# A two-layer decoder trunk for a prompt and eight samples: streams mixed by steps of one projection, samples' work in halves

## The chip, the cores and the metric

One core of a Trainium2 chip. The metric is the device time of one launch in microseconds (us). TensorE is PE below (PEld its weight loads), VectorE DVE, ScalarE ACT, GpSimd POOL; SP issues most of the DMAs. Every engine works through its own list of instructions in order and waits for semaphores of the others.

## The reference, cut to what matters

The trunk has two layers. It runs for a prompt of 1024 tokens and for 8 sample tokens that share all weights.

```python
def mem_attend(q, mk, mv):
    s = jnp.einsum('blhd,bmhd->bhlm', q, mk) * (q.shape[-1] ** -0.5)
    return jnp.einsum('bhlm,bmhd->blhd', jax.nn.softmax(s, axis=-1), mv)

def a_mixer(hn, w_in, lb, hg_gain, mem_k, mem_v, w_o, s0):      # layer 0
    q_h, f_h, i_h, g_h, q_m = jnp.split(hn @ w_in, 5, axis=-1)
    ...
    o, S = hgrn2_scan(q, k, v, logf, s0)       # state: S = f * S + k v, output q S
    o = rmsnorm(o, hg_gain) * jax.nn.silu(g_h)
    om = mem_attend(q_m, mem_k, mem_v)
    return jnp.concatenate([o, om], axis=-1) @ w_o, S

def b_mixer(...):                                               # layer 1
    os_ = stick_breaking(q_s, k_all, v_all, bias, q_pos, k_pos)
    om = mem_attend(q_m, mem_k, mem_v)
    return jnp.concatenate([os_, om], axis=-1) @ w_o

for l in range(DEPTH):
    hn = rmsnorm(h, g[0])
    mix = ...                                   # a_mixer or b_mixer
    h = h + rmsnorm(mix, g[1])
    h = h + rmsnorm(swiglu(rmsnorm(h, g[2]), w_gu[l], w_down[l]), g[3])
```

The samples have their own caches: 256 rows of memory keys and values each, a 128x128 state for each of 4 heads, and 256 past positions of the shared keys and values. The width is 1024, the inner width of the feed-forward part (FFN) 2816.

## The kernel before, in words

The prompt is cut into two groups of 512 tokens, 0 and 1; the 8 samples ride along as extra columns of group 1 (its matmuls are 260 columns wide, two of them for one of 512). Weights, and most activations, are split into a high and a low half (`ws`, by L208 on ACT and L209 on DVE, from a tile `w` that SP loads in L203), and a product of 128x128 weights is three matmuls. `proj` (L214 to L225, matmuls in L222) is one such projection: 24 matmuls of 512 columns for 8 blocks of input. Its result stands in one of two buffers `mm`; DVE and ACT take it out (`silu` with L247, L250 and L251, the gating product L819 and L230).

The order of the work is written as generators. Each `yield` ends a step, and `weave` (L178) always takes the next step of the stream that has made the smallest share of its weight: with weights 30, 50 and 24, for example, the three streams make 30, 50 and 24 steps in the same stretch. The instructions are recorded in that order and then placed on each engine by a scheduler; `tc.issue_after(split[0].ins)` tells it to place an instruction on DVE behind the last weight split made so far (L209, or L573 for Strassen slices).

The parts that the change touches:

- `ffn` (L800) computes the FFN by plain projections; a step of `part` is a gate and an up projection. `ffn_w` (L660) computes slices by Strassen's scheme: `gate_up_w` (L528) loads blocks with L538 into raw tiles, some of which lie in the buffers `b` that the attention parts use too, adds them on DVE (L557 to L565), splits them in L571 (ACT) and L573 (DVE) and multiplies in L578; its down projection is L751.
- `sample_scores` (L1037): for each sample a key tile `c` and a broadcast query row `b<-qd` are loaded, multiplied on DVE (L1057) and summed over each head (L1058) into `sc`. `mem_attn_sample` transposes `sc` on PE (L1125), makes the softmax (L1127 to L1132) and transposes back (L1135). `sample_pv` (L1063) multiplies the values (L1078), adds the two halves of the rows (L1079), splits and sums over partitions by L1069 on PE a sample later; it ends in L1087 and the transposes L1090.
- `hgrn_sample` (L1222): the samples' value rows are transposed, stored to memory (`vd`, L1229) and loaded again for each head as a broadcast over partitions (L1240, `c<-vd`), next to the state. On DVE the state is multiplied by the forget gate (L1253), the value rows by the key (L1254), the two are added (L1255), stored and multiplied by the query (L1257); split halves go to the matmuls L1262. The sum makes a round trip through memory (`od`, L1272) and is transposed in L1275.
- `sb_prompt` (L1490), stick-breaking attention of a group: scores L1501, biased evacuation L1512 to L1516, exponentials and logarithm L1487 and L1488 on ACT, a scan over positions L1521, L1523 and L1524, transposes L1530 and the products with values L1541. One block's transposes stand a step behind its scores.

The stages, in the order of the list of weaves: group 1 of layer 0 runs its recurrence beside `f0.part(0)`; its samples' state (`a1.sample`) and gate beside `f0.part(1)`; then its memory attention (`a1.mem`) and its samples' (`a1.mem_sample`) beside `f0.part(2)` and the first Strassen slices. In layer 1, group 0's attention runs beside two parts of Strassen slices, and group 1's beside its samples' attention and three parts of plain projections.

## Time and profile before

| what | us |
|---|---|
| median of 3 runs (2419.42 to 2420.16) | 2419.86 |
| the profiled execution's own time | 2420.19 |
| its span, first to last instruction | 2418.5 |
| PE busy | 2385.4 |
| DVE busy | 1732.6 |
| ACT busy | 1285.2 |

Matmuls overlap in the records (one of 512 columns is shown as 397 ns long, and starts about 233 ns after the one before), so a busy share of PE hides how well it is fed; waits and the granted clock in short stretches show more. In rows of time the columns are start, length, engine, line, operation, written tile and read tiles, shapes, and in brackets the idle time before and what ended it; `x13` stands for thirteen of a kind in a row. By the trace's time, the samples' state of layer 0 lies at about 506 to 622 us, the memory attention after it at 622 to 760 (the first Strassen slice begins at 752.75), the first stick-breaking group at 1000 to 1160 and the second at 1515 to 1905.

### The profile page before, as it was taken

The page shows a single profiled execution, that of the slowest core. Times are in us where ns is not written, and L with a number is a line of the kernel's source. Part 1 is how long each engine was busy: PE and PEld are TensorE (multiplying, and loading weights), DVE is VectorE, ACT ScalarE, POOL GpSimd, SP SyncE. Part 2 cuts the span into 40 slices and gives each one's busy share as a digit, 9 for nine tenths or more (in the row PEclk, how much of TensorE's full clock was granted, in tenths as well). Part 3 has the DMA queues.
Part 4 walks back from the last instruction along what each step waited for, and adds up shares of the span by engine and source line. Part 5 has one row for each costly group of instructions (what it writes and reads, how often), then busy time and mean ns, then how long its engine had stood idle before and what let it go on. Part 6 is the DMA issues. An engine that isn't in the chain of part 4 may idle for free. (4 is left out here: it accounts for less than half of the span.)

```text
span 2418.5 us, 42360 instructions
## 1 busy us (share of the span) xinstructions
PE 2385.4 (99%) x15959; PEld 2158.9 (89%) x15959; DVE 1732.6 (72%) x3218; ACT 1285.2 (53%) x2560; POOL 118.5 (5%) x187
## 2 busy tenths in 40 slices
PE   8999999999999999999999999999999999999998
PEld 6888988887779998899999989877778899999998
DVE  5867557665787676878566776788788678766866
ACT  5547544354445554666544554555554457554445
POOL 1000201110000000000002200021000000000000
PEclk9999999999999999999999999999999999999999
DMA  6454666577645446432568846455353353343342
GB/s 188 123 166 117 170 189 158 133 182 191 192 132 146 152 136 207 138 101 85 148 173 232 234 138 189 153 165 148 105 165 120 97 162 122 118 129 100 107 130 76
DMA packets 510991, 357.59 MB, mean 148 GB/s; under 512 B 20109, under 2 KB 459514, under 8 KB 510786
## 3 DMA queue, kind: packets, MB, share of 16 engines
q1 hardware_dynamic: 494914, 312.93, 43.4%
q0 software_dynamic: 15872, 41.95, 7.4%
q8 instruction: 126, 2.06, 0.3%
q14 instruction: 79, 0.65, 0.1%
HBM read 322.86 MB, written 65.49 MB: 161 GB/s over the span
## 5 line engine op out<-in xcount | busy, mean ns | idle before, releaser
L222 PE MATMUL mm<-x,ws 128*128 128x512 f32 (+1 forms) x5016 | 924.5, 342 | 5.3 <-DVE t L247 2.9
L222 PEld LDWEIGHTS mm<-x,ws 128*128 128x128 f32 x5016 | 776.6, 188 | 116.9 <-issue 3.7
L208 ACT CAST ws<-w 128x512 fp32r<-128x512 f32 x596 | 347.9, 585 | 433.1 <-PE mm L222 258.9
L209 DVE TENSOR_TENSOR ws<-w,ws 128x512 fp32r<-128x512 f32 x596 | 380.8, 644 | 223.7 <-ACT ws L208 218.8
L751 PE MATMUL q<-m,ws 128*128 128x260 f32 (+1 forms) x2496 | 306.3, 283 | 1.0 <-DVE ws L209 0.4
L751 PEld LDWEIGHTS q<-m,ws 128*128 128x128 f32 x2496 | 300.3, 188 | 3.4 <-ACT m L229 0.8
L578 PE MATMUL q<-y,ws 128*128 128x260 f32 (+1 forms) x1920 | 250.9, 284 | 1.5 <-ACT q L586 1.0
L578 PEld LDWEIGHTS q<-y,ws 128*128 128x128 f32 x1920 | 238.2, 188 | 3.7 <-ACT q L586 1.4
L578 PE MATMUL q<-x,ws 128*128 128x260 f32 (+1 forms) x1668 | 218.6, 283 | 0.2 <-DVE ws L573 0.2
L578 PEld LDWEIGHTS q<-x,ws 128*128 128x128 f32 x1668 | 207.4, 188 | 0.5 <-DVE ws L573 0.4
L222 PE MATMUL mm<-m,ws 128*128 128x512 f32 x768 | 194.1, 403 | 0.2 <-DVE r L414 0.2
L571 ACT CAST ws<-w 128x512 fp32r<-128x512 f32 x206 | 124.7, 618 | 98.0 <-PE q L751 33.0
L573 DVE TENSOR_TENSOR ws<-w,ws 128x512 fp32r<-128x512 f32 x206 | 139.2, 688 | 48.9 <-ACT ws L571 45.0
L222 PEld LDWEIGHTS mm<-m,ws 128*128 128x128 f32 x768 | 143.4, 190 | 32.0 <-DVE r L414 0.7
L760 DVE TENSOR_TENSOR r<-r,q 128x260 f32<-128x260 f32 (+1 forms) x160 | 60.7, 420 | 50.9 <-PE q L751 50.6
L504 PE MATMUL q<-x,ws 128*128 128x260 f32 (+1 forms) x720 | 89.7, 283 | 0.0
L504 PEld LDWEIGHTS q<-x,ws 128*128 128x128 f32 x720 | 87.5, 188 | 0.6
L571 ACT CAST ws<-b 128x512 fp32r<-128x512 f32 x82 | 50.5, 620 | 43.6 <-PE q L751 13.8
L229 ACT CAST m<-t 128x512 fp32r<-128x512 f32 (+1 forms) x88 | 54.8, 623 | 31.0 <-DVE t L619 13.2
L573 DVE TENSOR_TENSOR ws<-b,ws 128x512 fp32r<-128x512 f32 x82 | 56.2, 688 | 18.4 <-ACT ws L571 17.8
L230 DVE TENSOR_TENSOR m<-t,m 128x512 fp32r<-128x512 f32 (+1 forms) x88 | 60.6, 689 | 11.0 <-ACT m L229 10.2
L277 DVE TENSOR_TENSOR st<-st,n 128x512 f32<-128x512 f32 (+1 forms) x91 | 62.1, 690 | 3.6 <-ACT n L276 2.5
(411 smaller groups left out, 3094.4 us busy)
## 6 DMA issues: line engine op xcount, KB each, us to landing
w<-in_w_gu SPq DMA_DIRECT2D x275, 256.0 KB, 3.3
w<-in_w_down SPq DMA_DIRECT2D x160, 256.0 KB, 2.9
wsum<-in_w_gu POOLq DMA_DIRECT2D x48, 512.0 KB, 6.0
w<-in_w_in_a SPq DMA_DIRECT2D x80, 256.0 KB, 3.0
w<-in_w_o SPq DMA_DIRECT2D x64, 256.0 KB, 2.8
w<-wsum SPq DMA_DIRECT2D x61, 256.0 KB, 3.5
b<-in_w_gu SPq DMA_DIRECT2D x39, 256.0 KB, 3.3
b<-wsum SPq DMA_DIRECT2D x39, 256.0 KB, 4.0
```

The costliest lines, as they stand in the source:

```text
L208: nc.scalar.copy(ws[:, 0, :n, :], raw[:, :n, :])
L209: split[0] = nc.vector.tensor_sub(ws[:, 1, :n, :], raw[:, :n, :], ws[:, 0, :n, :].bitcast(F32))
L222: nc.tensor.matmul(ps[:, a, : PW[g]], wt, xt[k][:, xi, o : o + PW[g]], start=(k == 0 and wi == 0), stop=(k == nk - 1 and wi == 2),)
L229: nc.scalar.copy(dst[0], src)
L230: nc.vector.tensor_sub(dst[1], src, dst[0].bitcast(F32))
L277: nc.vector.tensor_add(acc[:, :n], acc[:, :n], t[:, :n])
L504: ins = nc.tensor.matmul(pp[a][:, :h], wt, xt[k][:, xi, a * h : (a + 1) * h], start=(k == 0 and wi == 0), stop=(k == ND - 1 and wi == 2),)
L571: nc.scalar.copy(w[:, 0, :], src)
L573: split[0] = nc.vector.tensor_sub(w[:, 1, :], src, w[:, 0, :].bitcast(F32))
L578: nc.tensor.matmul(ps[:, :h], w[:, wj, k * P : (k + 1) * P], x[:, xi, :], start=(first and k == 0 and wi == 0), stop=(k == 3 and wi == 2), ...
L751: nc.tensor.matmul(pp[a][:, :h], wt, mids[k][:, xi, a * h : (a + 1) * h], start=(k == 0 and wi == 0), stop=(k == nf - 1 and wi == 2),)
L760: nc.vector.tensor_add(d, d, pp[a][:, :h])
```

## The change

A step of `ffn.part` is now one projection (a `yield` between gate and up); a slice of `ffn_w.part` has two steps. `sample_scores` and `sample_pv` make two steps of each sample, with the second operation (reduction, addition) also tied behind a weight split. `value_rows` is taken out of `hgrn_sample` and runs a stage earlier (`a1.rows`); there the first state product is tied behind a split, each head takes two steps, the matmuls with its output stand a step later (`total`), and two steps lie between the loads of the round trip and its transposes. `mem_attn_sample`, `sample_pv` and the samples' stick-breaking get a few more steps, and the weights of the weaves are set anew.

```diff
                     next(slice_)
                     if late:
                         drain(late)
-                        yield
+                    yield
                     next(slice_)
                     late = slice_
-                    continue
                 yield
             if late:
                 drain(late)
...
                     nc.scalar.activation(sv(sg, g), pv(pg, g), AF.Silu)
                 else:
                     sg = silu(None, pg, g)
+                yield
                 pu = proj(g, w_gu[l], 0, ND, DFF + (f0 + j) * P, self.xt)
                 nc.vector.tensor_mul(sv(sg, g), sv(sg, g), pv(pu, g))
                 mt = M(F32R)
...
             nc.vector.tensor_scalar(Kd, Kd, oml[:, h : h + 1], None, op0=ALU.mult)
             yield
 
-    def hgrn_sample(Ft, Kt, Qt, vs):
+    def value_rows(vs, vd):
         pvv = S()
         for h in range(H):
             nc.tensor.transpose(pvv[:NB, h * P : (h + 1) * P], vs[:, h, :], ident)
         vT = B()
         nc.vector.tensor_copy(vT[:NB, :512], pvv[:NB, :])
-        vd = tc.dram_tile([NB, 512], F32, name=nm("vd"))
         nc.sync.dma_start(vd, vT[:NB, :])
         yield
+
+    def hgrn_sample(Ft, Kt, Qt, vd):
         HB = H * NB
         assert 2 * H == NB
 
...
         nxt = fetch(0)
         yield
         po = S()
+        late = []
+
+        def total():
+            for h, a, i, p in late:
+                nc.tensor.matmul(
+                    po[:NB, :], selr[:, 2 * h + a, :], p,
+                    start=(h == 0 and a == 0 and i == 0), stop=(h == H - 1 and a == 1 and i == 1),
+                )
+            late.clear()
+
         for h in range(H):
             def col(t):
                 return t[h // 2][:, h % 2, G : G + NB].unsqueeze(2).to_broadcast([P, NB, P])
...
             st, vb = nxt
             nxt = h < H - 1 and fetch(h + 1)
             stv, vbv = (t.rearrange("p a (b v) -> p (a b) v", v=P) for t in (st, vb))
-            nc.vector.tensor_mul(stv, stv, col(Ft))
+            with tc.issue_after(split[0].ins):
+                nc.vector.tensor_mul(stv, stv, col(Ft))
             nc.vector.tensor_mul(vbv, vbv, col(Kt))
             nc.vector.tensor_add(st, st, vb)
             nc.sync.dma_start(st_sample[0, :, h].rearrange("b k v -> k b v"), stv)
+            total()
+            yield
             nc.vector.tensor_mul(vbv, stv, col(Qt))
             for a in range(2):
                 qs = B(F32R), B(F32R)
                 split_to(qs, vb[:, a, :])
-                for i, p in enumerate(qs):
-                    nc.tensor.matmul(
-                        po[:NB, :], selr[:, 2 * h + a, :], p,
-                        start=(h == 0 and a == 0 and i == 0), stop=(h == H - 1 and a == 1 and i == 1),
-                    )
-            yield
+                late.extend((h, a, i, p) for i, p in enumerate(qs))
+            yield
+        total()
         rows = B()
         nc.vector.tensor_copy(rows[:NB, :], po[:NB, :])
         od = tc.dram_tile([H, NB, P], F32, name=nm("od"))
         nc.sync.dma_start(od.rearrange("h (a b) v -> (h a) b v", a=2), rows[:NB, :].rearrange("p (b v) -> p b v", v=P))
         ot = B()
         nc.sync.dma_start(ot[:NB, :].rearrange("p (h v) -> p h v", v=P), od.rearrange("h b v -> b h v"))
+        yield
+        yield
         pr = S()
         for h in range(H):
             nc.tensor.transpose(pr[:, h * NB : (h + 1) * NB], ot[:NB, h * P : (h + 1) * P], ident[:NB, :NB])
...
         def v(self):
             yield from v_proj(self.g, self.W, 8 * P, self.xt, self.V, self.vs)
 
+        def rows(self):
+            self.vd = tc.dram_tile([NB, 512], F32, name=nm("vd"))
+            yield from value_rows(self.vs, self.vd)
+
         def sample(self):
-            yield from hgrn_sample(self.F, self.K, self.Q, self.vs)
+            yield from hgrn_sample(self.F, self.K, self.Q, self.vd)
 
         def core(self):
             g = self.g
...
     weave((a0.mem(), 8), (a1.fq(), 8), (islice(w0, 12), 13))
     o0 = out_proj(0, 0, M)
     drain(o0.mm(a0.xo))
-    weave((o0.finish(), 17), (chain(a1.v(), a1.qm(A)), 8), (islice(w0, 12), 13))
+    weave((o0.finish(), 17), (chain(a1.v(), a1.rows(), a1.qm(A)), 9), (islice(w0, 12), 13))
     f0 = ffn(0, 0, o0.x)
-    weave((a1.core(), 22), (f0.part(0), 9), (islice(w0, 16), 17))
+    weave((a1.core(), 22), (f0.part(0), 14), (islice(w0, 16), 17))
     a1.open()
-    weave((a1.sample(), 6), (a1.gate(), 4), (f0.part(1), 9), (w0, 9))
+    weave((a1.sample(), 12), (a1.gate(), 4), (f0.part(1), 14), (w0, 9))
 
     def rest():
         yield from f0.part(2)
...
         yield from fw.part(4)
         f0.acc = fw.acc
 
-    weave((chain(a1.merge(), a1.mem()), 30), (a1.mem_sample(), 50), (rest(), 24))
+    weave((chain(a1.merge(), a1.mem()), 27), (a1.mem_sample(), 82), (rest(), 33))
     xk0, xb0 = [], []
     o1 = out_proj(1, 0, M)
     drain(o1.mm(a1.xo, 0, 1, True))
...
     b0.open(True)
     set_banks(True)
     fw = ffn_w(1, 0, o1.x, (5, 6, 5), 0, False, beside=(0, 1), src=o1.R)
-    weave((chain(b0.sb(), b0.mem()), 25), (chain(fw.part(0), fw.part(1)), 18))
+    weave((chain(b0.sb(), b0.mem()), 25), (chain(fw.part(0), fw.part(1)), 28))
     p4 = fw.part(4)
     back = b0.load()
     drain(fw.part(2), islice(back, 4))
-    weave((chain(fw.part(3), islice(p4, 4)), 8), (weight_sums(1, (4,)), 16))
+    weave((chain(fw.part(3), islice(p4, 8)), 20), (weight_sums(1, (4,)), 16))
     weave((p4, 4), (back, 8))
     f1 = ffn(1, 0, o1.x)
     f1.R, f1.acc = fw.R, fw.acc
...
     f0 = ffn(0, 1, o0.x)
     p3 = f0.part(3)
     weave(
-        (chain(b1.sb(), b1.mem()), 40), (chain(b1.sb_sample(), b1.mem_sample()), 39),
-        (chain(f0.part(0), f0.part(1), f0.part(2), islice(p3, 4)), 30),
+        (chain(b1.sb(), b1.mem()), 40), (chain(b1.sb_sample(), b1.mem_sample()), 76),
+        (chain(f0.part(0), f0.part(1), f0.part(2), islice(p3, 8)), 48),
     )
     o1 = out_proj(1, 1, A, True)
     fw = ffn_w(0, 1, o0.x, (), 4, False, f0.R, True)
...
         set_banks(True)
         yield from fw.part(4)
 
-    weave((o1.finish(), 17), (last(), 11))
+    weave((o1.finish(), 17), (last(), 13))
     f0.acc = fw.acc
     f1 = ffn_w(1, 1, o1.x, (5, 6, 5), 0, True)
-    weave((chain(f0.finish(False), store_y(0, f0.R), token_rows(1, o1.R)), 17), (chain(f1.part(0), f1.part(1)), 7))
+    weave((chain(f0.finish(False), store_y(0, f0.R), token_rows(1, o1.R)), 17), (chain(f1.part(0), f1.part(1)), 10))
     drain(f1.part(2), f1.part(3), f1.part(4))
 
 
```

In `sample_scores` the change reads (`sample_pv` has the same with its addition):

```diff
             with tc.issue_after(split[0].ins):
                 nc.vector.tensor_mul(kt, kt, qb.unsqueeze(1).to_broadcast([P, 2, 512]))
-            nc.vector.tensor_reduce(
-                scv[:, :, :, b], kt.rearrange("p k (h d) -> p k h d", h=H), axis=AX.X, op=ALU.add
-            )
+            yield
+            with tc.issue_after(split[0].ins):
+                nc.vector.tensor_reduce(
+                    scv[:, :, :, b], kt.rearrange("p k (h d) -> p k h d", h=H), axis=AX.X, op=ALU.add
+                )
             yield
```

What moves, at three places.

On SP's queue, where the samples' value rows `vd` are stored and first loaded again. Before, behind the recurrence (its end state is `out_st_prompt`):

```order
L203 DMA w_878_5362<-in_w_gu 128x4x128
L1407 DMA out_st_prompt<-carry_144 128x4x128
L203 DMA w_883_5399<-in_w_gu 128x4x128
L1229 DMA vd_854_5205<-b_853_5203 8x512
L203 DMA w_885_5404<-in_w_gu 128x4x128
L203 DMA w_892_5445<-in_w_gu 128x4x128
L1240 DMA c_891_5442<-vd_854_5205 128x8x128
L1240 DMA c_913_5595<-in_state_hgrn 128x8x128
L203 DMA w_894_5450<-in_w_gu 128x4x128
L1240 DMA c_914_5596<-vd_854_5205 128x8x128
```

Now, ahead of the recurrence, among the copies `hs0` of group 0's residual:

```order
L203 DMA w_658_4101<-in_w_gu 128x4x128
L403 DMA hs0_130<-m_499_3054 128x512
L203 DMA w_660_4106<-in_w_gu 128x4x128
L403 DMA hs0_130<-m_499_3054 128x512
L1235 DMA vd_611_3770<-b_613_3776 8x512
L203 DMA w_672_4170<-in_w_gu 128x4x128
L1248 DMA c_856_5208<-vd_611_3770 128x8x128
```

The store and the first load have moved some 45 issues ahead in the queue.

On PE, where the samples' scores `sc` are transposed (L1125, now L1131) after the last reduction. Before, with down projections (inputs `m`) on both sides:

```order
L222 MATMUL mm_6684<-m_6322,ws_6681 128x512 x3
L222 MATMUL mm_6684<-m_6418,ws_6681 128x512 x3
L222 MATMUL mm_6684<-m_6514,ws_6681 128x512 x3
L222 MATMUL mm_6684<-m_6610,ws_6681 128x512 x3
L1125 MATMUL s_6698<-ident,sc_6231 32x128 x2
L222 MATMUL mm_6749<-m_6322,ws_6746 128x512 x3
```

Now, behind the last up projection (inputs `x`):

```order
L222 MATMUL mm_6631<-x_3938,ws_6628 128x512 x3
L222 MATMUL mm_6631<-x_4006,ws_6628 128x512 x3
L222 MATMUL mm_6631<-x_4013,ws_6628 128x512 x3
L222 MATMUL mm_6631<-x_4077,ws_6628 128x512 x3
L1131 MATMUL s_6660<-ident,sc_6231 32x128 x2
L1010 MATMUL s_6670<-c_6493,a_3798 128x256 x2
```

The transposes have moved from between two down projections of 12 matmuls to the end of an up projection of 24.

On DVE, where the first Strassen slice begins: L573 makes the low halves `ws_1285` and on, `x_851` to `x_854` are outputs of the memory attention. Before:

```order
L573 TENSOR_TENSOR ws_1285_7554<-b_1284_7552,ws_1285_7554 128x512
L230 TENSOR_TENSOR a_1268_7450<-b_1270_7453,a_1268_7450 128x256
L230 TENSOR_TENSOR a_1268_7450<-b_1272_7457,a_1268_7450 128x256
L230 TENSOR_TENSOR a_1251_7328<-b_1271_7455,a_1251_7328 128x256
L573 TENSOR_TENSOR ws_1287_7572<-w_1286_7570,ws_1287_7572 128x512
L573 TENSOR_TENSOR ws_1289_7589<-b_1288_7587,ws_1289_7589 128x512
L573 TENSOR_TENSOR ws_1291_7607<-w_1290_7605,ws_1291_7607 128x512
```

Now:

```order
L1091 COPY b_1275_7519<-ns_1133_6735 8x512
L230 TENSOR_TENSOR m_1272_7507<-t_1254_7358,m_1272_7507 128x512
L230 TENSOR_TENSOR x_851_5203<-s_1279_7531,x_851_5203 128x8
L230 TENSOR_TENSOR x_852_5204<-s_1279_7531,x_852_5204 128x8
L230 TENSOR_TENSOR x_853_5205<-s_1279_7531,x_853_5205 128x8
L230 TENSOR_TENSOR x_854_5206<-s_1278_7528,x_854_5206 128x512
L230 TENSOR_TENSOR x_854_5206<-s_1279_7531,x_854_5206 128x8
L573 TENSOR_TENSOR ws_1285_7550<-b_1284_7548,ws_1285_7550 128x512
```

The slice's first split, which stood ahead of the last gated products and outputs, stands behind the samples' output columns (those of 8) and the last head's.

## What was predicted

> **What bounds the kernel now.** I read the page's busy times first, then the waits of the engine that is busy longest, then the stretches around those waits by granted clock, and last the rows of time on both sides of each wait.
>
> ```profile
> span 2418.5 us, 42360 instructions
> PE 2385.4 (99%) x15959; PEld 2158.9 (89%) x15959; DVE 1732.6 (72%) x3218; ACT 1285.2 (53%) x2560; POOL 118.5 (5%) x187
> ```
>
> PE bounds the whole span. The change takes no matmul away, so it can win only where PE stands still or runs at a lower clock. The waits of PE over the whole span:
>
> ```profile
> engine line waited for: us in total, times, longest us
> PE ns L363 <- DVE xtok L336: 9.7, 2, 8.1
> PE mm L222 <- DVE t L247: 2.9, 1, 2.9
> PE s L1125 <- DVE sc L1058: 2.9, 1, 2.9
> PE s L1530 <- ACT b L1524: 1.7, 7, 0.3
> PE s L1501 <- DVE b L1516: 1.4, 1, 1.4
> PE mm L222 <- DVE ws L209: 1.2, 2, 0.8
> PE s L1275 <- DMA b<-od: 0.5, 1, 0.5
> ```
>
> L363 is the head, which the change leaves alone. Two single waits of 2.9 us stand out, both behind DVE. What follows them is seen in the stretches (length, busy times, then the granted clock):
>
> ```profile
> core 0: us, PE busy (x) PEld busy (x) DVE busy (x) ACT busy (x) POOL busy (x), PEclk, DMA share, GB/s
> 556.00:562.00 6.00, 3.15 (x14) 2.28 (x13) 5.98 (x9) 1.46 (x3) 0.00 (x0) 1.00 0.77 177
> 562.00:566.00 4.00, 4.00 (x13) 3.10 (x12) 2.92 (x5) 3.03 (x7) 0.00 (x0) 0.57 0.93 297
> 566.00:622.00 56.00, 55.48 (x290) 45.73 (x288) 27.34 (x48) 22.65 (x41) 6.31 (x10) 1.00 0.62 163
> 674.00:678.00 4.00, 1.84 (x8) 1.15 (x7) 4.00 (x4) 0.62 (x1) 0.00 (x0) 1.00 0.00 1
> 678.00:685.00 7.00, 6.13 (x16) 4.06 (x16) 3.96 (x10) 0.58 (x3) 0.00 (x0) 0.51 0.73 222
> ```
>
> So each stop is followed by a stretch at a low clock: 0.57 over 4 us, which loses 4 x 0.43 = 1.7 us, and 0.51 over 7 us, which loses 7 x 0.49 = 3.4 us. That doubles what the table of waits shows.
>
> The clock is 1.00 during the stops and in the 56 us between, and low only right behind them. [...]
>
> **The samples' state (wait on L247).** DVE works in order, and one instruction holds it:
>
> ```profile
> 547.67 0.68 DVE L209 TENSOR_TENSOR ws<-w,ws 128x512 fp32r<-128x512 f32 x1
> 555.20 1.23 DVE L1254 TENSOR_TENSOR c<-c,a 128x1024 f32<-128x1024 f32 x1 [6.84 <-DMA c<-vd]
> 556.34 0.68 DVE L230 TENSOR_TENSOR m<-t,m 128x512 fp32r<-128x512 f32 x1
> ...
> 559.82 0.68 DVE L247 TENSOR_SCALAR t<-mm 128x520 f32<-128x520 f32 x1
> 560.65 6.66 PE L222 MATMUL mm<-x,ws 128*128 128x512 f32 x21 [2.85 <-DVE t L247]
> DMA to landing us min/median/max: 7.1/7.2/7.2
> ```
>
> L1254 waits 6.84 us for value rows that take 7.2 us to land, and L247, which would free PE's buffer, stands behind it. The change writes the rows to memory a stage earlier, so the first loads no longer queue behind weights, and it ties the state product to a weight split and takes its matmuls a step later. The loads of heads 2 and 3 still wait for a buffer; I count the work between the release and the product in the new order at more than 7.2 us by 2 us. I take the stop as gone with its low clock: -2.9 - 1.7 = **-4.6 us**. If a load is still late by more than that cover, up to all of it comes back; bound 0 to -4.6. The two steps put in behind the state's round trip through memory also take the 0.5 us of L1275: **-0.5**.
>
> **The samples' memory scores (wait on L1058).**
>
> ```profile
> 672.35 3.50 PE L222 MATMUL mm<-m,ws 128*128 128x512 f32 x14
> 673.93 2.36 DVE L1057 TENSOR_TENSOR c<-c,b 128x1024 f32<-128x1024 f32 x2 [1.03 <-DMA b<-qd]
> 676.21 2.34 DVE L1058 TENSOR_REDUCE sc<-c 128x8 f32<-128x1024 f32 x2
> 678.70 0.59 PE L1125 MATMUL s<-ident,sc 128*32 128x128 f32 x2 [2.85 <-DVE sc L1058]
> 624.78 20.58 PE L222 MATMUL mm<-x,ws 128*128 128x512 f32 x88
> ```
>
> Two products and two reductions of 1.2 us come together at the end, with one short down projection to cover them. One matmul of PE takes 20.58 / 88 = 0.234 us, so a gate or up projection of 24 takes 5.6 us. In the new order one whole such projection stands between the last reduction's issue and the transposes, and products and reductions alternate with the projections' own work. I take -2.9 - 3.4 = **-6.3 us**. Price if wrong: the two last operations are 2.4 us, less than the 5.6 us of cover, so I see no way to the full stop here. The softmax's second transposes now have some 4 us of PE work in place of 5.5 us in front of them: +0.4 (0 to 0.7).
>
> **What gets worse.** Three places.
>
> First, the beginning of the same scores. The query rows' load:
>
> ```profile
> 625.82 0.67 DVE L1047 COPY b<-s 8x512 f32<-8x512 f32 x1
> 633.29 1.23 DVE L1057 TENSOR_TENSOR c<-c,b 128x1024 f32<-128x1024 f32 x1 [0.55 <-DMA b<-qd]
> 635.14 1.23 DVE L1057 TENSOR_TENSOR c<-c,b 128x1024 f32<-128x1024 f32 x1 [0.63 <-DMA b<-qd]
> ```
>
> The first product starts 6.8 us after the end of the copy L1047, and waits; PE doesn't (its row of 88 matmuls runs through). In the new order L1047 stands at the start of a gate projection and ends about 1.0 us into it, so the first product starts at 7.8 us. Four products and three reductions (7 x 1.17 us), three evacuations (3 x 0.6), the second load's 0.6 and the split itself (0.6) follow before the weights of the third projection from there are split: 7.8 + 8.2 + 1.8 + 0.6 + 0.6 = 19.0 us, where PE wants the low half after three projections and two matmuls, 17.3. It is short by 1.7; between 0 (the loads land earlier) and 3 (the third load late too) I take the middle: **+1.5**.
>
> Second, the entry of the first Strassen slice, where the samples' tail now meets it. Durations:
>
> ```profile
> L571 ACT CAST ws<-b 128x512 fp32r<-128x512 f32 x5 | 3.1, 619 | 3.5 <-DMA b<-wsum 1.9 <-DMA b<-in_w_gu 1.6
> L573 DVE TENSOR_TENSOR ws<-b,ws 128x512 fp32r<-128x512 f32 x4 | 2.7, 684 | 1.7 <-ACT ws L571 1.7
> L230 DVE TENSOR_TENSOR x<-s,x 128x512 fp32r<-128x512 f32 x1 | 0.7, 683 | 0.0
> L229 ACT CAST x<-s 128x512 fp32r<-128x512 f32 x1 | 0.6, 579 | 0.0
> ```
>
> All seven splits L573 are done ahead of the slice now. In the new order the first stands behind the last output rows: PE ends L991, then L229 0.58, L571 0.62 on ACT, L230 and L573 0.68 each on DVE, the latter two partly beside; PE gets the high half after 0.58 + 0.2 + 0.62 + 0.2 = 1.6 us and the low half 0.7 us later. **+2.3** (0.5 if ACT takes the weight first; 6 if the slice's weights, whose buffers the samples' last tiles hold and which take 3.3 to 4 us to land, are late as well). One more activation table load falls on ACT there; ACT, 53% busy, hides it, and uncovered it would be one of these:
>
> ```profile
> 732.12 1.28 ACT L1021 ACT_TABLE_LOAD   x1 [0.63 <-DVE x L230]
> ```
>
> Third, the first stick-breaking group beside the first two Strassen parts (weight 18 becomes 28). A weight split there now stands behind a scan, its product and two biased evacuations:
>
> ```profile
> L1521 DVE TENSOR_TENSOR_SCAN b<-b,b 128x512 f32<-128x512 f32 x16 | 20.5, 1282 | 7.4 <-ACT b L1488 7.3
> L1523 DVE TENSOR_TENSOR b<-b,b 128x512 f32<-128x512 f32 x24 | 16.5, 687 | 0.3
> L1524 ACT ACTIVATE b<-b 128x512 f32<-128x512 f32 x24 | 15.2, 632 | 23.6 <-DVE b L1523 23.6
> L1488 ACT ACTIVATE b<-b 128x512 f32<-128x512 f32 x24 | 15.1, 631 | 0.0
> L1516 DVE TENSOR_SCALAR b<-s,biasp 128x512 f32<-128x512 f32 x16 | 11.9, 743 | 0.7 <-PE s L1501 0.7
> ```
>
> Scan, product and evacuation are 1.28 + 0.69 + 0.74 = 2.7 us; from 0 (its cover suffices) to 2.7, the middle: **+1.4**.
>
> **The second stick-breaking group** is the longest stage the change touches (its weave of three streams). By the same rows its chain from scores to transposes is 0.74 + 2 x 0.63 + 1.28 + 0.69 + 0.63 = 4.6 us and its handovers. Now its steps stand sometimes 11.2 us of PE apart and sometimes less than 1 us; in the new order every 5.6 us. PE's waits on L1530 and L1501 are 3.1 us in all; I let two thirds go: **-2.0** (-3.1 to 0 by these rows).
>
> **The sum.** -4.6 - 0.5 - 6.3 + 0.4 + 1.5 + 2.3 + 1.4 - 2.0 = -7.8 us. The profiled execution took 2420.19 us (span 2418.5 and 1.7 around it), 0.3 above the median of the three runs, 2419.86. So 2420.2 - 7.8 = 2412.4, and by the median **2412.1 us**.
>
> **Rivals.** (a) *The stops move*, chance 0.20. For it: loads of heads 2 and 3 are still issued only when a buffer comes free, and the first product waits in front of L819 and L247. If one 2.9 us stop turns up elsewhere and one new stop is followed by a low clock (3.4 us), it is 2412.1 + 6.3 = 2418. Against: each of the new stops I found is 2.3 us or less, and the span's other waits, up to 1.4 us, have no low clock beside them.
>
> (b) *More is won*, 0.13: the three new stops don't show and all 3.1 us of the second group go. 2419.9 - 4.6 - 0.5 - 6.3 - 3.1 = 2405. For it: PE's waits in the first group are now under half a microsecond each although DVE runs late there.
>
> (c) *Slower*, 0.17: in the second group the chain is met by the samples' halves. An evenly spaced chain has 5.6 - 4.6 = 1.0 us for its five handovers and anything of the samples; each sample half that falls inside adds 1.2 us and a weight split 0.64. Short by 1.2 + 0.64 - 1.0 = 0.84 us at each of 28 scans (24 whole and 4 short ones), PE loses 23.5 us: 2412.1 + 2.0 + 23.5 = 2438. It decides from about 12 of the 28 on (10 us). For it: twice as many sample steps, each tied behind a split, in a stage where DVE is the engine waited for. Against: the number of DVE operations is the same, and the halves spread them.
>
> (d) *The low clock is not the stops' own*, 0.05: the stretches at 0.57 and 0.51 come for another cause and stay. Then 2412.1 + 1.7 + 3.4 = 2417. [...] Against: both stand right behind a stop, and the 56 us after the first of them run at 1.00.
>
> **How the numbers follow.** The forecast, 2407 to 2415 by its own terms, has 0.45. What a measurement here can tell from no change is about 0.2%, 4.8 us: 2415.0 to 2424.7. The forecast (0.45) and (b) (0.13) are faster: 0.58; (a) and (d) are 0.25 and lie within it, and (c) is 0.17. The range takes in all of (a) and (d) and most of (b): 2404 to 2423.
>
> **What would show it.** L1254's and L1058's followers on PE no longer in the table of waits, and the clock at 1.00 after them: terms one and two. A wait of PE on L573 or L571 of 1.5 to 2.5 us where the Strassen slices begin; a wait on L209's splits of about 1.5 us after the first query load; waits in the second group under 2 us in sum. I am wrong if a granted clock near 0.5 still stands anywhere between 500 and 800 us, or if the second group's stage is longer than now.

## The result, and the profile after

| | before | changed | ratio, 95% interval |
|---|---|---|---|
| first measurement, 9 runs each: median us | 2418.93 | 2410.63 | 0.9972 (0.9962 to 0.9982) |
| second chip, 33 and 11 runs | 2417.29 | 2414.49 | 0.9989 (0.9980 to 0.9998) |
| third chip, 28 and 11 runs | 2416.92 | 2413.46 | 0.9986 (0.9977 to 0.9995) |
| profiled execution, first measurement: us | 2420.19 | 2413.43 | |
| its span, and mean granted clock | 2418.5, 0.997 | 2411.6, 0.998 | |

The changed kernel is faster in all three measurements, by 8.3 us in the first (forecast: 7.8) and by 2.8 and 3.5 us in the others. The second and third chip are different ones; which chip the first measurement was taken on is not known. The trace read here is the one of the first measurement, 6.9 us shorter in its span than the trace of before; the two others are compared with it where they differ.

The page's first lines of the changed kernel:

```profile
span 2411.6 us, 42315 instructions
PE 2379.0 (99%) x15959; PEld 2156.3 (89%) x15959; DVE 1734.8 (72%) x3220; ACT 1283.5 (53%) x2559; POOL 113.2 (5%) x187
```

The matmuls are the same 15959, and DVE has the same work. What moved is what PE waits for. Its waits in the changed kernel (line waiting, engine and line waited for, then the sum, the times and the longest):

```profile
engine line waited for: us in total, times, longest us
PE ns L363 <- DVE xtok L336: 10.2, 2, 7.9
PE s L1565 <- issue: 3.3, 2, 1.7
PE s L1554 <- ACT b L1548: 1.8, 4, 0.7
PE q L578 <- ACT ws L571: 1.8, 3, 1.3
PE mm L222 <- DVE ws L209: 1.5, 2, 1.0
PE mm L222 <- DVE t L819: 1.5, 1, 1.5
PE mm L222 <- DVE t L247: 1.2, 1, 1.2
PE q L578 <- DVE ws L573: 1.2, 3, 0.6
```

The two stops of 2.9 us are gone as such, the scores' one altogether. In their place stand several of 1 to 1.7 us: at the samples' state (L819 and L247), at the Strassen slice's entry (L571 and L573) and in the second stick-breaking group (L1565). The granted clock beside them, in stretches (start and end, length, busy times of the engines, then granted clock, DMA share and GB/s):

```profile
526.00:532.00 6.00, 4.52 (x20) 3.41 (x19) 3.38 (x4) 1.46 (x3) 0.50 (x2) 1.00 0.41 109
545.00:552.00 7.00, 5.82 (x26) 4.46 (x25) 4.21 (x5) 2.28 (x4) 0.00 (x0) 1.00 0.84 179
622.00:700.00 78.00, 77.54 (x349) 62.20 (x348) 72.11 (x115) 37.59 (x79) 0.00 (x0) 1.00 0.63 192
745.18:748.59 3.41, 1.84 (x14) 1.62 (x14) 2.74 (x6) 3.36 (x8) 0.00 (x0) 1.00 0.86 214
748.60:752.00 3.40, 3.40 (x18) 3.40 (x18) 3.29 (x6) 2.35 (x5) 0.00 (x0) 0.50 0.82 243
```

At the state and over the whole place of the scores (622 to 700) the clock is 1.00 now. Behind the slice's entry it is 0.50 for 3.41 us (748.59 to 752.00), which loses some 1.7 us in this execution (an estimate, 3.41 x 0.50). Over stretches of 4 us, 746 to 750 and 750 to 754, the same low clock reads as 0.82 and 0.75.

**The samples' state.** Rows of time of DVE and PE around its two stops, and the issues of the value rows on SP:

```profile
519.82 0.37 SPq L1248 DMA_DIRECT2D c<-vd  x1
540.45 0.37 SPq L1248 DMA_DIRECT2D c<-vd  x1
...
528.62 1.23 DVE L1273 TENSOR_TENSOR c<-c,a 128x1024 f32<-128x1024 f32 x1 [3.77 <-DMA c<-vd]
529.77 0.68 DVE L819 TENSOR_TENSOR t<-t,mm 128x512 f32<-128x512 f32 x1
547.79 1.23 DVE L1273 TENSOR_TENSOR c<-c,a 128x1024 f32<-128x1024 f32 x1 [4.43 <-DMA c<-vd]
548.93 0.69 DVE L247 TENSOR_SCALAR t<-mm 128x520 f32<-128x520 f32 x1
...
530.59 5.79 PE L222 MATMUL mm<-x,ws 128*128 128x512 f32 x24 [1.48 <-DVE t L819]
549.77 2.55 PE L222 MATMUL mm<-x,ws 128*128 128x512 f32 x10 [1.18 <-DVE t L247]
```

The chain is the old one, shorter: the loads of two heads are issued only when a buffer comes free (519.82 and 540.45) and are used 8.8 and 7.3 us later; DVE stands 3.77 and 4.43 us at the product, and the evacuation behind it keeps PE's buffer.

**The slice's entry.** PE, ACT and DVE where the first Strassen slice begins:

```profile
744.17 1.02 PE L991 MATMUL s<-b,c 128*128 128x256 f32 x4
746.46 0.50 PE L578 MATMUL q<-x,ws 128*128 128x256 f32 x2 [1.26 <-ACT ws L571]
747.27 1.45 PE L578 MATMUL q<-x,ws 128*128 128x256 f32 x10 [0.31 <-DVE ws L573]
745.23 0.66 ACT L229 CAST x<-s 128x512 fp32r<-128x512 f32 x2 [0.34 <-PE s L991]
745.77 0.63 ACT L571 CAST ws<-b 128x512 fp32r<-128x512 f32 x1
746.53 0.68 DVE L573 TENSOR_TENSOR ws<-b,ws 128x512 fp32r<-128x512 f32 x1
```

The weight's high half (L571) stands behind the last output rows (L229) on ACT, the low half behind both on DVE, as worked out ahead.

**The second stick-breaking group.** The two long stops there are new:

```profile
1551.83 1.23 DVE L1057 TENSOR_TENSOR c<-c,b 128x1024 f32<-128x1024 f32 x1 [0.49 <-DMA b<-qd]
1553.58 1.21 DVE L1060 TENSOR_REDUCE sc<-c 128x8 f32<-128x1024 f32 x1
1554.70 0.74 DVE L1540 TENSOR_SCALAR b<-s,biasp 128x512 f32<-128x512 f32 x1
1555.55 0.48 DVE L1562 MEMSET s<- 128x512 f32 x1
...
1556.14 1.13 PE L1565 MATMUL s<-b,a 128*128 128x128 f32 x8 [1.70 <-issue]
1755.97 1.13 PE L1565 MATMUL s<-b,a 128*128 128x128 f32 x8 [1.60 <-issue]
```

The profile names no releaser ("issue"). But the zeroing of the values' accumulator, L1562, ends at 1556.03 and PE starts at 1556.14; ahead of it on DVE stand a sample's product (L1057), its reduction (L1060) and an evacuation.

### The profile page after: what moved, and what is told of

The parts are those of the page before. It is cut to its first block, busy times and chain, and to the rows that moved or that the text cites. A ratio compares the mean times of both kernels' runs of the same rounds, so it can differ in the third digit from the quotient of the medians.

```text
span 2411.6 us, 42315 instructions
## 1 busy us (share of the span) xinstructions
PE 2379.0 (99%) x15959; PEld 2156.3 (89%) x15959; DVE 1734.8 (72%) x3220; ACT 1283.5 (53%) x2559; POOL 113.2 (5%) x187
## 4 chain that ended last, share of the span: by engine, by line
PE 51%; DVE 2%; ACT 2%; DMA 1%; issue 1%; DVEq 0%; SPq 0%; ACTq 0%
PE mm L222 17%; PE q L578 16%; PE q L750 10%; PE q L504 1%; PE s L1565 1%; PE s L1525 1%; PE q L782 1%; PE s L1010 1%; PE s L991 1%; PE s L1554 1%; DMA w<-in_w_in_b 0%; DVE x L230 0%; PE ns L1071 0%; PE s L978 0%; PE s L504 0%
## 5 line engine op out<-in xcount | busy, mean ns | idle before, releaser
L209 DVE TENSOR_TENSOR ws<-w,ws 128x512 fp32r<-128x512 f32 x596 | 380.9, 645 | 227.2 <-ACT ws L208 224.2
L750 PE MATMUL q<-m,ws 128*128 128x260 f32 (+1 forms) x2496 | 304.2, 282 | 0.4 <-DVE m L230 0.2
L750 PEld LDWEIGHTS q<-m,ws 128*128 128x128 f32 x2496 | 299.7, 188 | 1.6 <-ACT m L229 0.7
L578 PE MATMUL q<-y,ws 128*128 128x260 f32 (+1 forms) x1920 | 249.6, 284 | 0.5 <-ACT q L586 0.5
L578 PEld LDWEIGHTS q<-y,ws 128*128 128x128 f32 x1920 | 237.8, 189 | 1.6 <-ACT q L586 0.7
L578 PE MATMUL q<-x,ws 128*128 128x260 f32 (+1 forms) x1668 | 220.4, 283 | 3.0 <-ACT ws L571 1.6
L578 PEld LDWEIGHTS q<-x,ws 128*128 128x128 f32 x1668 | 207.8, 188 | 4.4 <-ACT ws L571 2.2
L222 PE MATMUL mm<-m,ws 128*128 128x512 f32 x768 | 187.2, 397 | 0.0
L571 ACT CAST ws<-w 128x512 fp32r<-128x512 f32 x206 | 125.1, 619 | 96.3 <-PE q L750 30.7
L573 DVE TENSOR_TENSOR ws<-w,ws 128x512 fp32r<-128x512 f32 x206 | 139.5, 688 | 44.7 <-ACT ws L571 43.4
L229 ACT CAST m<-t 128x512 fp32r<-128x512 f32 (+1 forms) x88 | 54.8, 623 | 49.0 <-DVE t L819 26.9
L571 ACT CAST ws<-b 128x512 fp32r<-128x512 f32 x82 | 50.5, 620 | 39.2 <-PE q L750 13.4
L573 DVE TENSOR_TENSOR ws<-b,ws 128x512 fp32r<-128x512 f32 x82 | 56.4, 688 | 17.8 <-ACT ws L571 15.9
```

The lines of the kernel that those rows point to most:

```text
L209: split[0] = nc.vector.tensor_sub(ws[:, 1, :n, :], raw[:, :n, :], ws[:, 0, :n, :].bitcast(F32))
L222: nc.tensor.matmul(ps[:, a, : PW[g]], wt, xt[k][:, xi, o : o + PW[g]], start=(k == 0 and wi == 0), stop=(k == nk - 1 and wi == 2),)
L229: nc.scalar.copy(dst[0], src)
L571: nc.scalar.copy(w[:, 0, :], src)
L573: split[0] = nc.vector.tensor_sub(w[:, 1, :], src, w[:, 0, :].bitcast(F32))
L578: nc.tensor.matmul(ps[:, :h], w[:, wj, k * P : (k + 1) * P], x[:, xi, :], start=(first and k == 0 and wi == 0), stop=(k == 3 and wi == 2), ...
```

## The experiments

The change has three parts that can be had apart: the new state of layer 0 (S), the samples' scores and values in halves (H), and FFN steps of one projection (F). Each experiment below is named by what it has of them or what it mends.

**Without the new state (H and F).** `hgrn_sample` as before, `a1.rows` gone:

```diff
-    weave((o0.finish(), 17), (chain(a1.v(), a1.rows(), a1.qm(A)), 9), (islice(w0, 12), 13))
+    weave((o0.finish(), 17), (chain(a1.v(), a1.qm(A)), 8), (islice(w0, 12), 13))
-    weave((a1.sample(), 12), (a1.gate(), 4), (f0.part(1), 14), (w0, 9))
+    weave((a1.sample(), 6), (a1.gate(), 4), (f0.part(1), 14), (w0, 9))
```

> The changed kernel with the samples' state as it was before (value rows stored in its own stage, one step a head, its matmuls at once, weight 6 for 12); all else as changed. Theory A (places): the stop behind the value rows' load comes back with its low clock: PE waits on L247 or L819 about 3 us at 545 to 560 us and the clock falls to about 0.5 to 0.6 for some 4 us, and L1275's 0.7 us returns; the changed kernel still has 3.0 us of stops there but no low clock, so this kernel is 2 to 3 us slower than the changed one (ratio to before about 0.998). Theory B (mixing): steps of one projection in all FFN parts keep PE fed and the place of the state doesn't matter: the same as the changed kernel within 1 us.

Measured: 2420.49 against 2417.14 us, 1.0017 (1.0007 to 1.0026). PE's wait at the state, and the stretch behind it:

```profile
PE mm L222 <- DVE t L247: 4.9, 1, 4.9
...
557.00:562.00 5.00, 4.74 (x12) 3.80 (x13) 5.00 (x9) 3.40 (x7) 0.00 (x0) 0.54 0.93 271
```

(This chip is called the fourth here; it is shared by the runs with whole samples, with the tail early and with the accumulator early.) So H and F without S are slower than before by 3.4 us, more than either theory expected. The old state beside projections of one step makes a stop of 4.9 us where it had made one of 2.9: PE runs out of work at 552.35, 5.4 us earlier than before (557.80), and the product with the value rows comes at nearly the same time (554.02, before 555.20). Without the new state, the rest costs time.

**Samples in whole steps (S and F).** `sample_scores` and `sample_pv` as before:

```diff
             with tc.issue_after(split[0].ins):
                 nc.vector.tensor_mul(kt, kt, qb.unsqueeze(1).to_broadcast([P, 2, 512]))
-            yield
-            with tc.issue_after(split[0].ins):
-                nc.vector.tensor_reduce(...)
+            nc.vector.tensor_reduce(...)
...
-(a1.mem_sample(), 82)
+(a1.mem_sample(), 48)
-(chain(b1.sb_sample(), b1.mem_sample()), 76)
+(chain(b1.sb_sample(), b1.mem_sample()), 44)
```

> The changed kernel with the samples' scores and values in whole steps again (product and reduction, product and addition in one step, no second tie), weights 48 and 44 for 82 and 76; the FFN's steps of one projection stay. Theory A: what was won at the end of the samples' scores was won by the halves; PE's stop of about 3 us in front of the scores' transposes returns with a low clock, +6 us against the changed kernel (ratio about 0.9997). Theory B: the finer FFN steps alone do it; no stop at the transposes, within 1 us of the changed kernel (0.997).

Measured: 2415.97 against 2417.14, 0.9995 (0.9986 to 1.0004): S and F without H gain nothing that can be told. The scores' transposes have no stop here either; F puts enough work in front of them. PE's wait on L1554's counterpart is 3.0 us in sum, where the three traces of the changed kernel have 1.3 to 2.8. The time is near the first theory's, the place is the second's: whether the halves add anything to S and F can't be told from this.

**The state in three steps a head.** The value rows' product a step later than the state's:

```diff
                 nc.vector.tensor_mul(stv, stv, col(Ft))
-            nc.vector.tensor_mul(vbv, vbv, col(Kt))
+            yield
+            with tc.issue_after(split[0].ins):
+                nc.vector.tensor_mul(vbv, vbv, col(Kt))
...
-(a1.sample(), 12)
+(a1.sample(), 16)
```

> The changed kernel with a third step in the samples' state: the value rows' product is issued a step after the state's own, tied behind a split, weight 16 for 12. Theory A: the value rows' load has one projection more (5.6 us) before DVE comes to it, so that the stops on L819 and L247 (1.0 to 3.0 us in the four profiles with the new state) go: 1 to 3 us less than the changed kernel of this call. Theory C: the loads are issued a step later too, since the buffers come free later: same stops, within 1 us.

Measured on the second chip, beside the changed kernel: 2415.16 and 2414.49, against before 0.9987 (0.9978 to 0.9996) and 0.9989 (0.9980 to 0.9998). Both state stops are gone, and the end of the first Strassen slices' stage comes 8.4 us earlier than in the trace of before, where the changed kernel on this chip had 5.5. It gives that back: from 1500 to 1920 it loses 4.0 us, 3.0 of them ahead of the second stick-breaking group, where PE waits 2.9 us for a weight split (its row below; the changed kernel on the same chip had 1.6 us on it in all) and the clock is low behind it (0.64 over 4 us). From its table of PE's waits:

```profile
PE mm L222 <- DVE ws L209: 4.4, 2, 2.9
```

**The samples' tail ahead of the slice.** Only weights:

```diff
-    weave((chain(a1.merge(), a1.mem()), 27), (a1.mem_sample(), 82), (rest(), 33))
+    weave((chain(a1.merge(), a1.mem()), 29), (a1.mem_sample(), 90), (rest(), 33))
```

> The changed kernel with weights 29 and 90 for 27 and 82 in the weave of memory attention, samples and Strassen slices, so that the samples end ahead of the first slice and all its splits stand ahead again. Theory A: the 2.0 us of waits at the first product L578 go and with them the low clock behind (0.82 and 0.75 over 4 us each, 1.7 us): 3.7 us less than the changed kernel (ratio about 0.9957). Theory C: the work is only moved and the stop shows up elsewhere in the stage: within 1 us of the changed kernel.

Measured: 2413.18 against 2417.14, 0.9979 (0.9970 to 0.9988). The stop at the slice's entry and the low clock behind it are gone; PE is busy through the stretch. Its row by stretches, and one of its waits of PE:

```profile
741.00:755.00 14.00, 14.00 (x118) 13.90 (x117) 7.54 (x14) 6.42 (x14) 0.00 (x0) 1.00 0.83 232
...
PE mm L222 <- DVE ws L209: 4.1, 2, 2.6
```

But the span, 2411.5, is that of the changed kernel's first trace. Of the 4.5 us won against that trace between 741 and 752, 2.8 are left at the end of that stage (PE waits 1.5 us at the first scores now) and 0.1 at the end of the span; the longest of the waits that took their place is the 2.6 us above, ahead of the second stick-breaking group. The changed kernel itself was not run on this chip, so whether the 2413.18 is a gain over it can't be told.

**The accumulator zeroed a step earlier.** In `sb_prompt`:

```diff
             for i, unit in enumerate(units):
+                if turned and turned[2] == 0:
+                    po[0] = S()
+                    nc.vector.memset(po[0], 0.0)
                 step(((h, vh, i), weights
...
-            if i == 0:
-                po[0] = S()
-                nc.vector.memset(po[0], 0.0)
```

> The changed kernel with the zeroing of the values' accumulator in stick-breaking issued a step earlier (the memset ahead of the next block's scores). Theory A: PE's two stops of 1.6 and 1.7 us in front of L1565, which the profile calls issue, are waits for that memset, which stands on DVE behind the samples' halves; they go, 3.3 us less (ratio about 0.9958). Theory D: they are PE's own issue and stay: within 1 us of the changed kernel.

Measured: 2412.08 against 2417.14, 0.9980 (0.9971 to 0.9989). L1565's row is gone from the waits, so the 3.3 us named "issue" were waits for the memset. Most of it turned into another wait in the same stage, which gained 1.2 us. The trace's span, 2408.8 us, is 2.8 us shorter than the changed kernel's first, but 2.2 us of that lead are there by 622 us, ahead of all that the edit touches: single traces of the same work differ by that much. The row of its table of PE's waits:

```profile
PE s L1554 <- ACT b L1548: 4.2, 6, 2.0
```

**FFN steps of two projections (S and H).** No `yield` between gate and up, the slices' steps and the weights of the FFN streams as before:

```diff
                     sg = silu(None, pg, g)
-                yield
                 pu = proj(g, w_gu[l], 0, ND, DFF + (f0 + j) * P, self.xt)
...
-(rest(), 33)
+(rest(), 24)
-(chain(f0.part(0), f0.part(1), f0.part(2), islice(p3, 8)), 48)
+(chain(f0.part(0), f0.part(1), f0.part(2), islice(p3, 4)), 30)
```

> The changed kernel with the FFN in pairs of projections again (no step between gate and up, a Strassen slice in one step) and its weights as before; samples' halves and state as changed. Theory A (halves): the scores' stop stays away without the finer FFN; within 2 us of the changed kernel. Theory B (mixing): the whole samples' steps had no stop with the finer FFN, so that the finer FFN is what took it away; here PE waits 2 to 3 us at the scores' transposes L1131 again, with a low clock, and the kernel is 4 to 6 us slower than the changed one.

Measured on the second chip: 2416.04 against 2417.29, 0.9996 (0.9987 to 1.0005). The scores' stop stays away, so either of H and F removes it. What is lost is in the second group: 7.2 us were won up to it in this trace, 2.2 remain at the end. From its table of PE's waits:

```profile
PE s L1565 <- DVE s L1562: 3.5, 2, 2.9
```

Here the profile itself names the memset L1562 as what L1565 waits for.

**The changed kernel again, second chip.** No edit.

> The changed kernel itself once more, as a measure for the others of this call: ratio 0.996 to 0.998 by its first runs. Its profile tells how much the stops at the samples' state (1.65 and 1.34 us in the first profile), the splits L209 and the head differ between executions of the same program; I expect the head's and the slice's to agree within 0.2 us and those behind a load of the value rows to differ by up to 1 us.

Measured: 0.9989 (0.9980 to 0.9998), 2.8 us, a smaller gain than the 0.996 to 0.998 expected. At the slice's entry PE has the same two stops (starts 1.52 and 0.47 us later than at the usual spacing, as in the first trace), now without a low clock behind; the low clock stands behind the state's stop instead. The row of PE at that stop, and three stretches, the last two at the slice's entry:

```profile
530.75 7.36 PE L222 MATMUL mm<-x,ws 128*128 128x512 f32 x24 [1.84 <-DVE t L819]
...
530.00:538.00 8.00, 7.25 (x25) 5.71 (x26) 6.95 (x11) 4.94 (x9) 0.92 (x2) 0.79 0.67 194
745.94:749.35 3.41, 2.02 (x14) 1.82 (x15) 2.94 (x6) 3.41 (x8) 0.00 (x0) 1.00 0.72 203
740.00:755.00 15.00, 13.43 (x101) 11.81 (x100) 9.58 (x20) 9.11 (x22) 0.00 (x0) 1.00 0.72 203
```

**The three mends together** (state in three steps, tail early, accumulator early):

```diff
+            yield
+            with tc.issue_after(split[0].ins):
+                nc.vector.tensor_mul(vbv, vbv, col(Kt))
...
-(chain(a1.merge(), a1.mem()), 27), (a1.mem_sample(), 82)
+(chain(a1.merge(), a1.mem()), 29), (a1.mem_sample(), 90)
...
+                if turned and turned[2] == 0:
+                    po[0] = S()
+                    nc.vector.memset(po[0], 0.0)
```

> Three mends together: the state in three steps, weights 29 and 90 for the samples' tail, the accumulator zeroed a step early. By the stops that each took away in its own profile (state 1 to 3 us, slice's entry 4.4 us at its place, less 1.1 at the first scores, zeroing 1.2 us for the stage) 5 to 7 us less than the changed kernel of this call, ratio to before about 0.9947. If the mends only move the waits: within 2 us of the changed kernel.

Measured: 0.9993 (0.9984 to 1.0002), on the second chip. Nothing adds up: a new stop appears at the memory keys, and the second group's wait on ACT grows. From its table of PE's waits:

```profile
PE s L1556 <- ACT b L1550: 6.4, 7, 1.9
PE s L1010 <- DMA c<-mks: 2.5, 1, 2.5
```

**Only the finer FFN steps (F).** The edits of the first two experiments together (the few added steps of the samples' streams, and the weights of the other weaves, stay):

```diff
-(a1.sample(), 12)
+(a1.sample(), 6)
...
-(a1.mem_sample(), 82)
+(a1.mem_sample(), 48)
-(chain(b1.sb_sample(), b1.mem_sample()), 76)
+(chain(b1.sb_sample(), b1.mem_sample()), 44)
```

> The finer FFN steps and their weights alone: samples' state, scores and values in whole steps as before. If the parts add up (place marks of the first profiles: state 5.5 us, samples' halves 2.6 us of the changed kernel's 6.8): 1 us slower than before, ratio 1.000 to 1.001, with a stop of some 5 us on L247 at the samples' state and none at the scores' transposes. If the mixing is what the change lives from: 0.998 or less.

Measured on the third chip: 2424.30 against 2416.92, 1.0029 (1.0016 to 1.0041). From its table of PE's waits, and the stretch behind the first of them:

```profile
PE mm L222 <- DVE t L247: 5.0, 1, 5.0
PE s L1544 <- issue: 3.3, 3, 1.9
...
556.00:562.00 6.00, 4.50 (x11) 3.62 (x12) 6.00 (x9) 3.33 (x6) 0.00 (x0) 0.52 0.93 257
```

F alone is slower, by 7.4 us, where adding up the parts had given 1. The old state's stop is 5.0 us with a clock of 0.52 behind it, and the second group has its new stops (L1544 is the values' product here) with whole samples too. F brings them as H does.

**Only the new state (S).** The kernel before with the new `hgrn_sample` and `a1.rows`:

```diff
-    weave((o0.finish(), 17), (chain(a1.v(), a1.qm(A)), 8), (islice(w0, 12), 13))
+    weave((o0.finish(), 17), (chain(a1.v(), a1.rows(), a1.qm(A)), 9), (islice(w0, 12), 13))
-    weave((a1.sample(), 6), (a1.gate(), 4), (f0.part(1), 9), (w0, 9))
+    weave((a1.sample(), 12), (a1.gate(), 4), (f0.part(1), 9), (w0, 9))
```

> The kernel before with the samples' state of the change alone (rows stored a stage earlier, two steps a head, matmuls a step later, two steps behind the round trip). If the state's own place is what wins: its stop of 3.0 us and the low clock behind it (1.7 us) and L1275's 0.7 shrink to 1 to 3 us of stops, 2 to 4 us less than before, ratio 0.9985; the scores' stop of 3.0 us and its low clock stay. If the state needs the finer FFN steps to hide the load: no gain, ratio 1.000.

Measured on the third chip: 2412.78 against 2416.92, 0.9984 (0.9975 to 0.9993), as much as the whole change has there. DVE's products with the loaded value rows, the waits of PE, and the stretch of the state:

```profile
526.31 1.23 DVE L1266 TENSOR_TENSOR c<-c,a 128x1024 f32<-128x1024 f32 x1 [2.34 <-DMA c<-vd]
553.56 1.23 DVE L1266 TENSOR_TENSOR c<-c,a 128x1024 f32<-128x1024 f32 x1 [1.84 <-DMA c<-vd]
...
PE s L1125 <- DVE sc L1058: 2.7, 1, 2.7
PE s L1547 <- ACT b L1541: 1.7, 7, 0.3
PE s L1518 <- DVE b L1533: 1.4, 1, 1.4
...
526.00:566.00 40.00, 40.00 (x197) 32.76 (x197) 30.53 (x43) 20.15 (x34) 4.34 (x7) 1.00 0.74 198
```

DVE still waits for the value rows, but only 2.34 and 1.84 us, and PE is busy through all 40 us: no stop and no low clock. The stop at the scores is left (2.7 us), and the second group's waits are near those of before (1.7 and 1.4 us).

**The changed kernel a third time**, beside these two.

> The changed kernel a third time, as the measure of this call: ratio 0.997 to 0.999 by its first two (0.9972 and 0.9989, whose intervals just meet).

Measured: 0.9986 (0.9977 to 0.9995), 3.5 us. Its trace has the state's stop at L819 (1.60 us) and the slice's stop, neither with a low clock, and single waits of 1.4 to 1.6 us that the first trace doesn't have (L209, L266 and L750).

**The state in three steps and the accumulator early**, without the third mend:

```diff
+            yield
+            with tc.issue_after(split[0].ins):
+                nc.vector.tensor_mul(vbv, vbv, col(Kt))
...
+                if turned and turned[2] == 0:
+                    po[0] = S()
+                    nc.vector.memset(po[0], 0.0)
```

> The state in three steps and the accumulator zeroed a step early, without the new weights for the samples' tail, behind which the three mends had a new stop of 2.7 us on a key load. If the two mends keep what each won at its place (3 us at the state, 1.2 us in the second stick-breaking stage): 3 to 4 us less than the changed kernel of this call. If the second stage takes back what comes earlier, as it did with the state in thirds (4 us back there): within 1.5 us of the changed kernel.

Measured: 2414.66 against 2416.92, 0.9990 (0.9981 to 0.9999). No gain over the changed kernel on the same chip (2413.46); the memset's stop is gone, L1556 waits 5.2 us and L209 4.3 instead, and the clock is 0.88 over 741 to 755 us, where the changed kernel's trace on this chip has 1.00; over the whole span it is 0.997 against 0.999.

The parts side by side, each against before on its own chip (each interval is 2 to 3 us to either side; the rows stand on different chips):

| S | H | F | us | ratio |
|---|---|---|---|---|
| x | | | -4.1 | 0.9984 |
| | | x | +7.4 | 1.0029 |
| | x | x | +3.4 | 1.0017 |
| x | | x | -1.2 | 0.9995 |
| x | x | | -1.3 | 0.9996 |
| x | x | x | -2.8, -3.5 (first measurement -8.3) | 0.9989, 0.9986 (0.9972) |

H alone was not run.

## Why the prediction was right, and where not

**The total.** 2410.63 us against a forecast of 2412.1, inside the forecast's own 2407 to 2415. Two further measurements give ratios that put the same kernel at 2419.86 x 0.9989 = 2417.2 and 2419.86 x 0.9986 = 2416.5: inside the range, but where rivals (a) and (d) were, and with less than half of the gain that was forecast. The sign and the range are well supported; that the first measurement met the forecast gain to half a microsecond is luck in good part. The terms beside the first trace, by the time at which PE starts the same matmul in the order of its work:

| stretch, in the time of before | forecast, us | first trace, us |
|---|---|---|
| up to 622: state, round trip | -5.1 | -2.1 |
| 622 to 760: scores, slice's entry | -2.1 | -2.4 |
| 760 to 1500: first stick-breaking group | +1.4 | -1.9 |
| 1500 to 1920: second group | -2.0 | +0.4 |
| the rest | 0 | -0.9 |
| sum | -7.8 | -6.9 |

Errors of 2 to 3 us cancel. In the two other traces of the changed kernel the third row is +1.3 and +1.5 us, by the waits on L266 and L750.

**The signs.** The prediction named two signs that it is wrong: a clock near 0.5 anywhere between 500 and 800 us, and a longer second group. Both came in the first trace: 0.50 from 748.59 to 752.00, and 0.4 us. The number held; the account of where the time goes held only in part.

**The low clock's size.** The terms of the state and the scores hold 5.1 us of low clock, read from one execution of the kernel before. That execution lost 6.6 us to the clock over its whole span (an estimate, half of the stretches at 0.50: 562.11 to 565.52, 678.16 to 684.99 and 2415.55 to 2418.48). The 95 later executions on the second, third and fourth chip lost 4.7 to 4.9 us on average, and the changed kernel's 22 on the second and third 3.1 to 3.3 (an estimate from the mean granted clocks, which are kept to three decimals). So what the change takes from the low clock is nearer 1.5 us on average than 5.1: this part of the two terms is over-sized, by a trace that was not an average one.

**The state, -4.6: mis-sized.** In the first trace the low clock went (1.7 us) and the stop of 2.85 turned into 1.48 + 1.18, so about -1.9. The step that failed is "I count the work between the release and the product in the new order at more than 7.2 us by 2 us". The product came 8.8 and 7.3 us after the issue, and DVE had been idle for 3.77 and 4.43 us of it, so the cover was some 5.0 and 2.9 us, and the first of the two loads took longer than the 7.2 us counted on. With the old FFN steps the new state did what was forecast, or more: that trace gains 5.7 us between the recurrence and L1275 (from 0.2 late to 5.5 early against before), where the two terms of state and round trip made 5.1. So S by itself did not fail. What differs with F is at the first stop not a shorter cover (5.0 us, with S alone 3.9) but later rows: 8.8 us from issue to use in the first trace, 6.2 us with S alone. At the next load the cover is shorter with F (2.9 us against 5.0). Why the rows come later was not tried. In the two runs without S, F makes the old state's stop 4.9 to 5.0 us, because PE runs out of work earlier.

**The round trip `od`, -0.5: right**; its row is gone from the table of waits.

**The scores, -6.3: right at the place.** No wait at their transposes, clock 1.00 over 622 to 700. The second transposes' +0.4 did not show. But not H by itself did it: F or H each suffices.

**The first scores, +1.5: too high in this trace.** One wait on L209 of 0.5 us between 622 and 700, as before. On the third chip it was 1.43 us, on the second 0.7. The bounds held in all three.

**The slice's entry, +2.3: right,** 1.26 and 0.31 us of wait in the rows, 2.0 us by the starts of the matmuls, by the chain of L229, L571 and L573 that was worked out. The 0.2 us that the sum takes for each handover is an estimate: in the rows L571 ends at 746.40 (745.77 + 0.63) and PE starts at 746.46; in the trace of before L247 ends at 560.50 (559.82 + 0.68) and PE starts at 560.65. Not foreseen is the low clock behind it, 1.7 us in one of the three traces of the changed kernel. That is a piece of rival (a); its condition "each of the new stops I found is 2.3 us or less" was no protection.

**The first stick-breaking group, +1.4: not seen.** PE's longest wait between 1000 and 1200 is 0.6 us; its cover suffices, which was the lower bound.

**The second group, -2.0: wrong, the step that failed.** I let two thirds of 3.1 us go. The old waits did shrink (1.4 on L1501 is gone), but L1565 now waits 3.3 us for the zeroing of its accumulator behind a sample's product and reduction, so the stage is no shorter: the gain over before is 6.4 us in front of it and 6.0 behind. The prediction followed the chain from scores to transposes and left out the memset, a small operation at the start of each head, that is queued on DVE as well. Zeroing earlier removes exactly these stops, but gives 2.2 us back at the chain's own wait on L1548 (3.4 us in the stage, against 1.2): DVE's order is so tight there that a wait moved is not a wait removed. By 0.4 us the stage is longer; that is far from the 23.5 us of rival (c). The samples' work does hold PE up there, at 2 places in the stage and not at 12.

**Rivals (b) and (d).** Three small stops showed, so (b) did not come. Nor did (d): where the stops went (the scores; the state with S alone), the clock stayed at 1.00 in these traces.

**What the change lives from.** On the third chip S alone gives what the whole change gives. H and F remove the scores' stop, 6.3 us at its place in the first trace, and pay most of it back at the state (2.1 us won there against 5.5 with S alone) and at the slice's entry (some 4 us back); the span of the trace with S alone, 2411.8 us, is that of the whole change. Where the further 5 us of the first measurement come from stays open: its trace differs from the third chip's by waits of 1 to 2 us (on L209, L266 and L750), the intervals of the ratios meet, and there is only one trace of before.

## What to carry to other kernels

A finer interleave can remove a stop by putting other work in front of it, and it can shorten the cover of other waits in the same stretch: price each wait beside the change again, with the new step's length, not only the one it aims at. Take the size of a low clock from many executions: one trace can lose more to it than the average one (6.6 us here, against 4.7 to 4.9). When following a chain, list the small operations on the same engine as well (a memset, a copy): here the price of a memset of 0.48 us was the work queued in front of it, 3.3 us of waits that the profile names "issue". Where several parts are changed together, run each alone before crediting the sum: here one part of three gave the gain on the chip where it was run alone, one was a loss by itself, and the mends that were run beside the changed kernel won 3 us at their place and nothing at the end.

## What the runs showed of the hardware

In the trace of before the clock is 0.50 from 562.11 to 565.52 and from 678.16 to 684.99, and 1.00 over 556 to 562, 566 to 622 and 685 to 700; the 0.57 and 0.51 of the prediction are means over longer stretches. The first of the two begins 1.5 us after PE has started again (560.65). The second begins 0.5 us before the scores' transposes (678.70), while PE still stands, where the prediction read the clock as low only behind the stops. In the two runs with the old state and F the clock is low during the stop as well: 0.81 over 551 to 557 us with H and F, 0.89 over 551 to 556 with F alone.

In the low stretch of the first trace PE's matmuls come more slowly: the 22 of L578 from 748.55 on, most of them at 0.50, take 4.28 us, the 12 behind them 1.58.

```profile
748.55 4.28 PE L578 MATMUL q<-a,ws 128*128 128x256 f32 x22
752.67 1.58 PE L578 MATMUL q<-x,ws 128*128 128x256 f32 x12
```

The length of a stop alone did not tell whether a low clock came with it. At 2.50 us (the memory keys, three mends) the clock is 0.60 over 641 to 645 us, and at 2.89 us (L209, state in three steps) 0.64 over 1499 to 1503. At 2.63 us (L209, F alone) it is 1.00 over 648 to 656, and at 2.60 us (L209, tail early) 1.00 over 1499 to 1507. The changed kernel's stops at the slice's entry have a clock of 0.50 behind them in the first trace and 1.00 in the two others (741 to 760 us); its stop at the state has 1.00 in the first trace (1.48 us) and in the third chip's (1.60 us), and 0.79 over 530 to 538 us in the second chip's (1.84 us). What decides it was not shown.

A load's time from issue to use was not constant either, where DVE waited for it: the value rows of the same head were used 6.2 us after the issue with S alone (520.08 to 526.31) and 8.8 us in the changed kernel (519.82 to 528.62). What lengthens it was not tried.

```profile
520.08 0.37 SPq L1241 DMA_DIRECT2D c<-vd  x1
```
